# The front's products of a streaming-encoder layer: one fp32 matmul per product in place of three fp32r passes over split halves

## The chip, the cores and the metric

The kernel runs on one core of one Trainium2 chip. The metric is device time in microseconds of one execution; the runs shown are of one program on one core. TensorE does the matrix products, VectorE, ScalarE and GpSimd the elementwise work, and SyncE (SP) issues the loads. Times "at" some microsecond count from the first instruction of the profiled execution.

## What is computed

One layer of an encoder on 256 tokens of 1024 features, all in fp32:

```python
x = layer_norm(x, ln_in_g, ln_in_b)
h = x @ w_in[l] + b_in[l]                       # 1024 -> 5640 columns
fq, fk, fv, ff, hq, hf, hi, hg, gates = split_cols(h, IN_SIZES)
...
y_fox = from_heads(fox_o) @ w_fox_branch[l]     # attention with forget gates, 8 heads of 64
...
y_hgrn = o @ w_hgrn_branch[l]                   # gated linear recurrence, 8 heads of 64
g = jax.nn.sigmoid(gates)
mixed = (g[..., :D_MODEL] * y_fox + g[..., D_MODEL:] * y_hgrn) @ w_mix_out[l] + b_mix_out[l]
x = layer_norm(ALPHA * x + mixed, ln1_g[l], ln1_b[l])
y_moe = grouped_top2_moe(x, ...)                # 16 experts, two chosen for each token
x = layer_norm(ALPHA * x + y_moe, ln2_g[l], ln2_b[l])
```

## The kernel before, in words

**Two parts.** The front is everything up to the first norm and the router: the input products, the two branches and the output projection, with the token mixer's work in between. The experts follow, two at a time, 64 slots for the tokens of each. The experts' 201 MB of weights are loaded once, in the order of use, into every slot that comes free.

**Tiles of the front.** The front's weights are 15 tiles of 128 x 4096 (2 MB each), numbered by `KIND` and loaded into a ring of three slots (`load_front`, line 81); the last tile has a place of its own. A tile is eight units of 512 columns. Tiles of kind "tm" (0, 3, 6 on the input, 13 and 14 for the output) give tokens on partitions: the operand is stationary and 512 columns of weights move, for two halves of tokens, so a unit has two products. Tiles of kind "fm" (1, 2, 4, 5, 7 to 10 on the input) and "f4" (11 and 12, the branches) give features on partitions: 128 x 128 of weights are stationary and 256 tokens move, four products to a unit.

**Three passes.** `prep(u)` (line 154) splits a unit of weights: `hi` is its rounding to fp32r, by ScalarE (line 164; three units by VectorE, line 162), `lo` is what is left, by VectorE or GpSimd (line 165, chosen by `on_pool`). The operands are split in the same way: the input by `x_hi` and `x_lo` (lines 244 to 249), the branches' by `feat_split` and `f_split`, the output's by `mix_split`. A product is then three matmuls into one bank of PSUM (`mm`, lines 185 to 187 and 198 to 200). The cumulated forget gates (`f_sum`, lines 675 and 678) use the same trick.

**The order.** TensorE, VectorE, ScalarE and GpSimd run in the order of the code. The loop at line 1065 makes steps 2 to 59 of two units each: `pe[i]` before the step's first products, evacuations of finished products and `post[i]` after them, then `prep` for units ahead, then the second unit. `pe`, `mid` and `post` hold the mixer's work, put at its steps with `at`. Steps 8 to 11 are tile 2, steps 12 to 15 are tile 3, and so on. Steps 16 to 23 carry the recurrence, step 24 a branch on a value that all engines read (line 594), steps 29 to 40 the attention. VectorE evacuates tile 0 (`ev_hv`, line 374), which frees two of the four banks that products use, and tile 2 (`ev_hq`, line 384); for tile 1 it works on SBUF alone (lines 379 and 380). GpSimd prepares the residual in seven sweeps over 128 x 1024 (`resid`, lines 317 to 322), placed at steps 4 to 9.

**Loads.** SP issues loads in an order of its own, which the scheduler decides; a load waits for its slot. `load_front` is called for the next tile when a tile has been used (steps 3, 7, 11, ...), `load_exp` and `load_parts` for the experts. Slots for experts come free as the front goes on: four at steps 16 to 29, one at step 40, the mixer's operands at steps 48 and 52 (`phase5`, `phase6`), the gates' at step 53 (`phase7`), the ring's, and the input's and the last tile's from step 56 on (`last_parts`). `warm` and `warm1` are products without use, over waits.

Of the kernel before, what the change touches and what calls it, by code (L numbers as in the profile page):

```python
# [35 lines left out]
# columns of the row pack  # L36
# [10 lines left out]
def trunk(ctx: ExitStack, tc: tile.TileContext, x, cst_d, rows_d, wf, we, lvl_d, out):  # L47
# [98 lines left out]
    # ---- products in three passes of exact halves; a unit: 512 columns of a weight tile  # L146
    KIND = ["tm", "fm", "fm", "tm", "fm", "fm", "tm", "fm", "fm", "fm", "fm", "f4", "f4", "tm", "tm"]
    split = {}
    NU = 8 * len(KIND)

    def on_pool(u):
        return u in (0, 1, 2) or 24 <= u < 56 and u % 2 == 1 or u >= 56 and u % 4 == 3

    def prep(u):
        if u >= NU:
            return
        c = u % 8
        src = fr[u // 8][c // 2][:, c % 2 * 512:c % 2 * 512 + 512] if u >= NU - 8 else fr[u // 8][:, c * 512:c * 512 + 512]
        hi = HI.tile([128, 512], F32R, name="hi", tag="hi")
        lo = HI.tile([128, 512], F32R, name="lo", tag="lo")  # L160
        if u in (6, 28, 30):
            V.tensor_copy(hi, src)
        else:
            A.copy(hi, src)  # L164
        (G if on_pool(u) else V).tensor_sub(lo, src, hi.bitcast(F32))  # L165
        split[u] = hi, lo
# [5 lines left out]
    def mm(u, tts=(0, 1)):  # L172
        i, c = u // 8, u % 8
        hi, lo = split[u]
        rh, rl = operands[i]()
        if KIND[i] == "tm":
            for tt in tts:
                if c == 0:
                    # the very last sums in two banks, so that their ends can overlap
# [43 lines left out]
    def x_turn(tt, j):  # L223
        """two blocks of features, a bank each pair"""
# [6 lines left out]
    def x_affine(tt, j):  # L231
        p = xq[tt, j]
        if j == 0:
            xq["t", tt] = P2.tile([128, 8, 128], F32, name="xt", tag="hk" if tt else "lf")
        xt = xq["t", tt][:, 2 * j:2 * j + 2, :]
        for i in range(2):
            k = slice(2 * j + i, 2 * j + i + 1)
            if j % 2 == 0:
                V.tensor_scalar(xt[:, i, :], p[:, i, :], C("ing")[:, k], C("inb")[:, k], op0=OP.mult, op1=OP.add)
            else:  # L240
                A.activation(xt[:, i, :], p[:, i, :], AF.Identity, bias=C("inb")[:, k], scale=C("ing")[:, k])
        xq[tt, j] = xt

    def x_hi(tt, j):
        A.copy(xt4[j][:, 0, :, tt * 128:(tt + 1) * 128], xq[tt, j])

    def x_lo(tt, j):
        t = slice(tt * 128, (tt + 1) * 128)
        (G if j == 3 or (tt, j) == (1, 1) else V).tensor_sub(xt4[j][:, 1, :, t], xq[tt, j],
                                                             xt4[j][:, 0, :, t].bitcast(F32))  # L250

    operands = {i: (lambda: xp) for i in range(11)}
    def x_parts(tt, j):
        x_affine(tt, j)
        x_hi(tt, j)
        x_lo(tt, j)
# [11 lines left out]
    prep(0)  # L268
    prep(1)
    x_affine(0, 0)  # L270
    x_affine(0, 1)
    x_stats(1)
    x_hi(0, 0)
    x_hi(0, 1)
    x_lo(0, 0)
    mm(0, (0,))
    V.bn_aggr(mvs(1), sm[:, 24:36])
    x_lo(0, 1)
    mm(1, (0,))
    prep(2)  # L280
# [3 lines left out]
    prep(3)  # L284
    x_turn(1, 0)
    x_turn(1, 1)
    mm(2, (0,))
    mm(3, (0,))
    x_affine(1, 0)
    x_norm(1, 1)  # L290
    x_affine(1, 1)
    x_hi(1, 0)
    x_hi(1, 1)
    x_lo(1, 0)
    x_lo(1, 1)
    mm(0, (1,))
    x_turn(1, 2)
    x_turn(1, 3)
    mm(1, (1,))
    x_affine(0, 2)  # L300
    x_hi(0, 2)
    x_lo(0, 2)
    mm(2, (1,))
    prep(4)
    x_affine(1, 2)
    x_hi(1, 2)
    x_lo(1, 2)
    mm(3, (1,))
    prep(5)
    x_parts(0, 3)  # L310
    prep(6)
    x_parts(1, 3)
    prep(7)

    # residual with the output bias: alpha * (x * g + b) + b_mix
# [8 lines left out]
    # lower bounds of the forget gates: cumsum(softmax) - its first row, over one layer  # L324
# [4 lines left out]
    Ur = PB.tile([128, 256], F32R, name="ur")  # L329
# [25 lines left out]
    def small3():  # L355
        V.tensor_copy(Ur, U)

    # tensors of the mixer
# [48 lines left out]
    # ---- HGRN2  # L407
# [7 lines left out]
    def hgrn_general(oh):  # L415
        """the same scores for any decays: pairs of tokens by the highest bit in which they differ;
        every exponent is at most zero"""
# [3 lines left out]
        for j in range(4):  # L421
# [38 lines left out]
            # between chunks: from the end of the key's chunk to the start of the query's  # L460
# [43 lines left out]
    def h_exps(j):  # L504
# [7 lines left out]
        # half of the chunk's decay as the reference point: exponents of both signs, at most  # L512
        # half the decay; beyond SAFE the general path below recomputes the scores
# [6 lines left out]
        # between chunks: from the key's reference point to the query's  # L520
# [18 lines left out]
    # two heads side by side: each on its half of the tensor engine's rows  # L539
# [21 lines left out]
    def transposed(p, val, sts, j):  # L561
        """two heads' sums of values: features on partitions, the scores' keys there too"""
# [51 lines left out]
    def feat_pe(ot):  # L614
        """[tokens, 512] to features on partitions"""
# [5 lines left out]
    def feat_split(p, o, tt):  # L621
        t = slice(tt * 128, (tt + 1) * 128)
# [990 lines left out]
```

## Time and profile before

| | us |
|---|---|
| median of 3 runs | 703.58 |
| lowest and highest | 702.56, 705.85 |
| profiled execution, span from first to last instruction | 704.5 |
| TensorE busy | 661.4 (94%) |
| VectorE, ScalarE, GpSimd busy | 210.1, 188.5, 93.1 |
| read from HBM | 236.95 MB, 338 GB/s over the span |

Of the profiled execution the span is the only time on record, and it stands for that execution's own time below. Busy time of TensorE is the union of modelled durations, which overlap from one matmul to the next, so it says that an engine has work, not that it is at its peak. The chain of waits follows the end back to what released each step. Stretches with their busy times, the granted clock and the load queue's share tell the stages apart; a clock of 1.00 is 2.4 GHz and one of 0.50 is 1.2 GHz. "f32" stands for fp32 and fp32r alike in a matmul's shapes; the tiles' names tell them apart (`hi`, `lo`, `xp`, `mp` are fp32r).

### The profile page before, as it was taken

The page shows a single profiled execution, that of the slowest core. Times are in us where ns is not written, and L with a number is a line of the kernel's source. Part 1 is how long each engine was busy: PE and PEld are TensorE (multiplying, and loading weights), DVE is VectorE, ACT ScalarE, POOL GpSimd, SP SyncE. Part 2 cuts the span into 40 slices and gives each one's busy share as a digit, 9 for nine tenths or more (in the row PEclk, how much of TensorE's full clock was granted, in tenths as well). Part 3 has the DMA queues.
Part 4 walks back from the last instruction along what each step waited for, and adds up shares of the span by engine and source line. Part 5 has one row for each costly group of instructions (what it writes and reads, how often), then busy time and mean ns, then how long its engine had stood idle before and what let it go on. Part 6 is the DMA issues. An engine that isn't in the chain of part 4 may idle for free.

```text
span 704.5 us, 9357 instructions
## 1 busy us (share of the span) xinstructions
PE 661.4 (94%) x3707; PEld 388.1 (55%) x3707; DVE 210.1 (30%) x457; ACT 188.5 (27%) x389; POOL 93.1 (13%) x83
## 2 busy tenths in 40 slices
PE   6779998999999999999999999999999999699986
PEld 5678797899998953534534443443443433243433
DVE  5776862654468521100100100100100100100015
ACT  4536354577645421102012010010010010010211
POOL 2632344433136000000000000000000000000001
PEclk8979999999999999999999999999999999999999
DMA  8926633543978969999999999999999999999981
GB/s 330 382 105 225 270 121 123 194 178 118 360 287 300 397 206 375 425 394 429 425 407 424 421 412 421 424 412 421 420 417 419 418 420 416 418 425 410 412 331 60
DMA packets 40520, 238.75 MB, mean 339 GB/s; under 512 B 4496, under 2 KB 4624, under 8 KB 32400
## 3 DMA queue, kind: packets, MB, share of 16 engines
q1 hardware_dynamic: 40464, 238.02, 84.3%
q8 instruction: 33, 0.54, 0.3%
q14 instruction: 23, 0.19, 0.1%
HBM read 236.95 MB, written 1.05 MB: 338 GB/s over the span
## 4 chain that ended last, share of the span: by engine, by line
PE 67%; DMA 13%; DVE 2%; ACT 0%; issue 0%; DVEq 0%; SPq 0%; ACTq 0%
PE g L1276 25%; DMA w<-in_we_dram 13%; PE g L1293 13%; PE g L1248 3%; PE g L198 3%; PE g L199 3%; PE g L200 3%; PE acc L1301 3%; PE g L186 1%; PE g L187 1%; PE g L185 1%; PE g L1312 1%; PE g L1422 1%; PE g L1284 1%; PE g L1116 1%; DVE e L1465 1%
## 5 line engine op out<-in xcount | busy, mean ns | idle before, releaser
L1276 PE MATMUL g<-w,e 128*64 128x512 f32 x992 | 219.7, 595 | 2.4 <-DMA w<-in_we_dram 2.4
L1276 PEld LDWEIGHTS g<-w,e 128*64 128x64 f32 x992 | 69.0, 137 | 138.6 <-issue 125.8
L1293 PE MATMUL g<-w,f 128*64 128x512 f32 x448 | 106.5, 604 | 2.4 <-DMA w<-in_we_dram 2.4
L165 DVE TENSOR_TENSOR lo<-w,hi 128x512 fp32r<-128x512 f32 x85 | 69.1, 824 | 62.1 <-ACT hi L164 61.3
L164 ACT CAST hi<-w 128x512 fp32r<-128x512 f32 x117 | 70.4, 620 | 54.2 <-PE g L199 39.3
L198 PE MATMUL g<-xp,hi 128*128 128x256 f32 x256 | 76.3, 298 | 9.0 <-DVE hv L374 9.0
L199 PE MATMUL g<-xp,hi 128*128 128x256 f32 x256 | 74.2, 290 | 0.0
L200 PE MATMUL g<-xp,lo 128*128 128x256 f32 x256 | 74.0, 289 | 0.0
L1293 PEld LDWEIGHTS g<-w,f 128*64 128x64 f32 x448 | 39.2, 138 | 59.5 <-issue 54.5
L1523 POOL TENSOR_TENSOR e<-e,par 128x256 f32<-128x256 f32 x2 | 1.4, 726 | 459.4 <-DVE nmr L1519 459.4
L165 POOL TENSOR_TENSOR lo<-w,hi 128x512 fp32r<-128x512 f32 x35 | 47.4, 1357 | 109.6 <-ACT hi L164 109.6
L198 PEld LDWEIGHTS g<-xp,hi 128*128 128x128 f32 x256 | 50.8, 199 | 11.3 <-issue 10.4
L199 PEld LDWEIGHTS g<-xp,hi 128*128 128x128 f32 x256 | 50.9, 199 | 0.1
L200 PEld LDWEIGHTS g<-xp,lo 128*128 128x128 f32 x256 | 50.8, 199 | 0.0
L1479 DVE COPY f<-g 128x512 f32<-128x512 f32 x7 | 4.8, 692 | 115.2 <-PE g L1293 115.2
L1248 PEld LDWEIGHTS g<-e,raw 128*128 128x128 f32 x224 | 26.1, 191 | 19.8 <-DVE e L1240 10.0
L1248 PE MATMUL g<-e,raw 128*128 128x128 f32 x224 | 28.7, 281 | 8.1 <-DVE e L1240 8.1
L1259 ACT ACTIVATE e<-g,cst 128x128 f32<-128x128 f32 x28 | 10.6, 457 | 68.7 <-PE g L1248 68.7
L1463 DVE TENSOR_TENSOR e<-e,g 128x512 f32<-128x512 f32 x8 | 5.5, 688 | 73.5 <-ACT e L1462 73.5
L185 PE MATMUL g<-hi,xp 128*128 128x512 f32 x48 | 20.7, 431 | 6.5 <-PEq L594 3.4
L1471 ACT COPY f<-g 128x512 f32<-128x512 f32 x8 | 4.7, 586 | 79.9 <-PE g L1284 79.9
L1301 PE MATMUL acc<-f,e 128*128 128x512 f32 x56 | 25.9, 605 | 0.0
(318 smaller groups left out, 745.5 us busy)
## 6 DMA issues: line engine op xcount, KB each, us to landing
w<-in_we_dram SPq DMA_DIRECT2D x49, 2048.0 KB, 17.7
w<-in_we_dram SPq DMA_DIRECT2D x178, 512.0 KB, 10.4
w<-in_wf_dram SPq DMA_DIRECT2D x13, 2048.0 KB, 8.4
w<-in_wf_dram SPq DMA_DIRECT2D x8, 512.0 KB, 9.1
w<-in_we_dram SPq DMA_DIRECT2D x16, 256.0 KB, 6.0
rbc<-in_rows_dram SPq DMA_DIRECT2D x1, 1036.0 KB, 15.9
f<-in_we_dram SPq DMA_DIRECT2D x4, 256.0 KB, 7.6
out_dram<-par SPq DMA_DIRECT2D x4, 256.0 KB, 2.1
```

What stands on the lines that cost most here:

```text
L164: A.copy(hi, src)
L165: (G if on_pool(u) else V).tensor_sub(lo, src, hi.bitcast(F32))
L185: PE.matmul(p, rh(c)[:, t], hi[:, a:b], start=c == 0, stop=False, skip_group_check=True)
L186: PE.matmul(p, rh(c)[:, t], lo[:, a:b], start=False, stop=False, skip_group_check=True)
L198: PE.matmul(p, hi[:, w], rh(k), start=k == 0, stop=False)
L199: PE.matmul(p, hi[:, w], rl(k), start=False, stop=False)
L200: PE.matmul(p, lo[:, w], rh(k), start=False, stop=k == nk - 1)
L1248: PE.matmul(p[:, i, :], raw[:, tt, k * 128:(k + 1) * 128], oneh2[:, tt, :], start=tt == 0, stop=tt == 1)
L1259: A.activation(t[:, i, :], p[:, i, :], AF.Identity, bias=C("b1")[:, 4 + i:5 + i], scale=C("g1")[:, 4 + i:5 + i])
L1276: PE.matmul(h[64 * nh:64 * nh + 64, :], xg[kh][:, k, 64 * (e % 2):64 * (e % 2) + 64], wcol(e, m + kh, k, nh), start=kh + k == 0, stop=kh = ...
L1293: PE.matmul(py[nh][64 * a:64 * a + 64, :], hT[a][:, c0:c0 + 64], wt[:, nh * 512:nh * 512 + 512], start=f == 0, stop=f == 7)
L1301: PE.matmul(acc[tt][nh], GT[:, tt, :], y[nh], start=start, stop=False, skip_group_check=True)
```

## The change

Products take weights and operands as they are, in fp32, one matmul each. `prep`, `on_pool`, `halves`, `x_hi`, `x_lo`, `mix_split` and `small3` are gone. The normed input is written once, into two tiles (`xT`) instead of four. The branches' operands are one copy each (`feat_put`, `f_put`), and the output takes the gated sum where it lies, in `gates`. At the start, the second half of the tokens is prepared in one go, between the first four units' products for the first half and for the second. Everything else keeps its step.

```diff
     KIND = ["tm", "fm", "fm", "tm", "fm", "fm", "tm", "fm", "fm", "fm", "fm", "f4", "f4", "tm", "tm"]
...
-    def prep(u):
-        if u >= NU:
-            return
+    def wunit(u):
         c = u % 8
-        src = fr[u // 8][c // 2][:, c % 2 * 512:c % 2 * 512 + 512] if u >= NU - 8 else fr[u // 8][:, c * 512:c * 512 + 512]
-        hi = HI.tile([128, 512], F32R, name="hi", tag="hi")
-        lo = HI.tile([128, 512], F32R, name="lo", tag="lo")
-        if u in (6, 28, 30):
-            V.tensor_copy(hi, src)
-        else:
-            A.copy(hi, src)
-        (G if on_pool(u) else V).tensor_sub(lo, src, hi.bitcast(F32))
-        split[u] = hi, lo
+        return fr[u // 8][c // 2][:, c % 2 * 512:c % 2 * 512 + 512] if u >= NU - 8 else fr[u // 8][:, c * 512:c * 512 + 512]
...
                 for p, a in tmp[tt]:
-                    b = a + 512 // len(tmp[tt])
-                    PE.matmul(p, rh(c)[:, t], hi[:, a:b], start=c == 0, stop=False, skip_group_check=True)
-                    PE.matmul(p, rh(c)[:, t], lo[:, a:b], start=False, stop=False, skip_group_check=True)
-                    PE.matmul(p, rl(c)[:, t], hi[:, a:b], start=False, stop=c == 7, skip_group_check=True)
+                    PE.matmul(p, x_of(c)[:, t], w[:, a:a + 512 // len(tmp[tt])], start=c == 0, stop=c == 7,
+                              skip_group_check=True)
...
         for kk in range(4):
-            k, w = k0 + kk, slice(kk * 128, (kk + 1) * 128)
-            PE.matmul(p, hi[:, w], rh(k), start=k == 0, stop=False)
-            PE.matmul(p, hi[:, w], rl(k), start=False, stop=False)
-            PE.matmul(p, lo[:, w], rh(k), start=False, stop=k == nk - 1)
+            k = k0 + kk
+            PE.matmul(p, w[:, kk * 128:(kk + 1) * 128], x_of(k), start=k == 0, stop=k == nk - 1)
...
-    def halves(name):
-        """exact halves of eight blocks of features, in four parts"""
-        t = [X.tile([128, 2, 2, T], F32R, name=name, tag="w", bufs=4) for _ in range(4)]
-        return [lambda k, i=i: t[k // 2][:, i, k % 2, :] for i in range(2)], t
-
-    xp, xt4 = halves("xp")
+    xT = [X.tile([128, 4, T], F32, name="xT", tag="w", bufs=4) for _ in range(2)]
+
+    def x_of(k):
+        return xT[k // 4][:, k % 4, :]
...
     def f_sum(j):
...
-            for part in range(2):
-                PE.matmul(pF[:, hh], lfr[:, part, h:h + 1].to_broadcast([128, 128]), Ur,
-                          start=part == 0, stop=False)
-            for part in range(2):
-                PE.matmul(pF[:, hh, 1], lfr[:, part, 8 + h:9 + h].to_broadcast([128, 128]),
-                          Ur[:, 0:128], start=False, stop=part == 1)
+            PE.matmul(pF[:, hh], f[:, 2, h:h + 1].to_broadcast([128, 128]), U, start=True, stop=False)
+            PE.matmul(pF[:, hh, 1], f[:, 2, 8 + h:9 + h].to_broadcast([128, 128]), tri, start=False, stop=True)
...
-    operands[11] = lambda: [lambda k, i=i: oH[i][:, k, :] for i in "hl"]
-    operands[12] = lambda: [lambda k, i=i: oF[i][:, k, :] for i in "hl"]
-    operands[13] = operands[14] = lambda: late["mp"]
+    operands[11] = lambda k: oH["o"][:, k, :]
+    operands[12] = lambda k: oF["o"][:, k, :]
+    operands[13] = operands[14] = lambda k: late["gates"][:, k, :]
...
-        if i > 2:
-            prep(2 * i + 3)
...
-        prep(2 * i + 4)
```

How the instructions move, at three places. On TensorE, at the start (line 127 is `warm`, 228 and now 207 the turning of the input, `g`, `s`, `o` are banks), the first products of tile 0 stood before like this:

```order
L127 MATMUL s<-hst_116 128x128 x2
L185 MATMUL g<-hi,xp 128x512
L186 MATMUL g<-lo,xp 128x512
L187 MATMUL g<-hi,xp 128x512
L185 MATMUL g<-hi,xp 128x512
L186 MATMUL g<-lo,xp 128x512
L187 MATMUL g<-hi,xp 128x512
L228 MATMUL g<-cst,raw 128x128 x2
```

and now, up to the end of tile 2 (line 169 is a product of 512 columns, 181 one of 256, 566 and 577 belong to the forget gates):

```order
L127 MATMUL s<-hst_116 128x128 x2
L169 MATMUL g<-w,xT 128x512 x4
L207 MATMUL g<-cst,raw 128x128 x2
L207 MATMUL s<-cst,raw 128x128 x2
L207 MATMUL o<-cst,raw 128x128 x2
L207 MATMUL g<-cst,raw 128x128 x2
L169 MATMUL g<-w,xT 128x512 x12
L181 MATMUL g<-xT,w 128x256 x8
L566 MATMUL g<-xT,wff 32x128 x16
L181 MATMUL g<-xT,w 128x256 x8
L577 MATMUL g<-cst,ffs 128x128 x2
L181 MATMUL g<-xT,w 128x256 x48
```

Each triple has become one row's count, on `w` and `xT` themselves; the four turnings of the second half stand together.

On VectorE, around steps 4 to 8 (`lbt` are the lower bounds, `hv`, `lf`, `hk` the evacuations of tiles 0 and 1, `ff` the forget gates), before:

```order
L343 TENSOR_SCALAR lbt<-cst 128x4
L165 TENSOR_TENSOR lo<-w,hi 128x512 x2
L374 TENSOR_TENSOR hv<-g,rbc 128x512 x2
L165 TENSOR_TENSOR lo<-w,hi 128x512 x2
L379 TENSOR_SCALAR lf<-lf,lbt 128x256
L380 TENSOR_SCALAR hk<-hk,lbt 128x256
L165 TENSOR_TENSOR lo<-w,hi 128x512 x2
```

and now, up to the first evacuations of tile 2 (`hqt`):

```order
L276 TENSOR_SCALAR lbt<-cst 128x4
L304 TENSOR_TENSOR hv<-g,rbc 128x512 x2
L309 TENSOR_SCALAR lf<-lf,lbt 128x256
L310 TENSOR_SCALAR hk<-hk,lbt 128x256
L309 TENSOR_SCALAR lf<-lf,lbt 128x256
L310 TENSOR_SCALAR hk<-hk,lbt 128x256
L582 TENSOR_REDUCE ff<-g 128x16
L583 TENSOR_TENSOR ff<-ff,rbc 128x16
L585 TENSOR_SCALAR ff<-ff 128x16
L586 TENSOR_TENSOR ff<-ff 128x16
...
L314 SCALAR_TENSOR_TENSOR hqt<-g,cst,hqt 128x256 x4
```

The splits between the evacuations are gone; left out are four more rows of 309 and 310.

On SP, the loads after the third weight tile (128x4096 from `in_wf` is a front tile, `in_we` are experts' weights), before:

```order
L99 DMA in_bmix<-in_rows_dram 128x1024
L84 DMA w<-in_wf_dram 128x4096 x4
L891 DMA w<-in_we_dram 128x1024 x3
L84 DMA w<-in_wf_dram 128x4096
L891 DMA w<-in_we_dram 128x1024
L864 DMA w<-in_we_dram 128x4096
L84 DMA w<-in_wf_dram 128x4096 x2
```

and now:

```order
L99 DMA in_bmix<-in_rows_dram 128x1024
L84 DMA w<-in_wf_dram 128x4096 x2
L804 DMA w<-in_we_dram 128x1024
L84 DMA w<-in_wf_dram 128x4096
L804 DMA w<-in_we_dram 128x1024 x3
L777 DMA w<-in_we_dram 128x4096
L84 DMA w<-in_wf_dram 128x4096
L804 DMA w<-in_we_dram 128x1024 x2
L84 DMA w<-in_wf_dram 128x4096 x3
```

The first expert loads stand two front tiles earlier, and two parts more come before tile 6, in what the input's split halves used to take.

## Rows read from the trace of the kernel before

**Rows 1.** Page, the chain that ended last: shares of the span by engine.

```profile
PE 67%; DMA 13%; DVE 2%; ACT 0%; issue 0%; DVEq 0%; SPq 0%; ACTq 0%
```

**Rows 2.** The chain in order of time: start us, us, what.

```profile
251.09 1.87 PE g L1422 x8
...
589.55 10.18 DMA w<-in_we_dram
...
676.35 4.47 DMA w<-in_we_dram
```

**Rows 3.** By stretch: us; PE, PEld, DVE, ACT, POOL busy; clock, DMA share, GB/s.

```profile
0.00:32.00 32.00, 25.97 (x148) 21.14 (x148) 21.09 (x42) 18.45 (x38) 13.52 (x22) 0.89 0.92 363
32.00:63.50 31.50, 23.09 (x171) 23.12 (x172) 23.77 (x37) 12.27 (x25) 11.01 (x5) 0.84 0.36 135
63.50:181.00 117.50, 111.81 (x838) 100.10 (x836) 67.53 (x180) 71.05 (x158) 44.12 (x36) 0.97 0.50 187
181.00:239.30 58.30, 58.07 (x420) 54.43 (x419) 35.91 (x60) 29.03 (x50) 21.58 (x18) 1.00 0.85 324
239.30:282.00 42.70, 42.70 (x243) 23.27 (x243) 12.23 (x51) 10.55 (x18) 0.00 (x0) 0.96 0.83 310
282.00:590.00 308.00, 301.07 (x1432) 124.65 (x1430) 31.62 (x52) 33.04 (x73) 0.00 (x0) 1.00 1.02 418
```

**Rows 4.** TensorE in order of time, products of 256 columns.

```profile
189.73 0.28 PE L198 MATMUL g<-xp,hi 128*128 128x256 f32 x1
...
190.09 0.28 PE L198 MATMUL g<-xp,hi 128*128 128x256 f32 x1
```

**Rows 5.** TensorE in order of time, products of 512 columns; the last begins tile 3.

```profile
21.71 0.39 PE L185 MATMUL g<-hi,xp 128*128 128x512 f32 x1
...
22.39 0.39 PE L185 MATMUL g<-hi,xp 128*128 128x512 f32 x1
...
63.46 0.40 PE L185 MATMUL g<-hi,xp 128*128 128x512 f32 x1
```

**Rows 6.** TensorE in order of time, fp32 matmuls of the experts; x2 covers both.

```profile
311.36 0.59 PE L1301 MATMUL acc<-f,e 128*128 128x512 f32 x1
...
311.36 1.02 PE L1301 MATMUL acc<-f,e 128*128 128x512 f32 x2
...
689.12 0.70 PE L1319 MATMUL acc<-f,e 128*128 128x256 f32 x2
```

**Rows 7.** Groups by shape, TensorE: count, busy us, mean ns, idle before.

```profile
L198 PE MATMUL g<-xp,hi 128*128 128x256 f32 x256 | 76.3, 298 | 9.0 <-DVE hv L374 9.0
...
L185 PE MATMUL g<-hi,xp 128*128 128x512 f32 x48 | 20.7, 431 | 6.5 <-PEq L594 3.4 <-ACT xp L245 3.1
```

**Rows 8.** TensorE's waits up to 250 us: total, times, longest.

```profile
PE g L198 <- DVE hv L374: 9.0, 1, 9.0
PE g L185 <- PEq L594: 3.4, 1, 3.4
...
PE o L577 <- DVE hst L558: 1.5, 1, 1.5
...
PE g L186 <- DVE lo L165: 0.9, 2, 0.7
```

**Rows 9.** VectorE and GpSimd in order of time, during the residual's sweeps.

```profile
33.95 2.34 POOL L322 TENSOR_TENSOR raw<-raw,in_inb 128x1024 f32<-128x1024 f32 x1
34.01 2.31 DVE L343 TENSOR_SCALAR lbt<-cst 128x4 f32<-128x4 f32 x1
...
39.19 2.69 POOL L322 TENSOR_TENSOR raw<-raw,in_inb 128x1024 f32<-128x1024 f32 x1
```

**Rows 10.** Page, costliest groups: the splits of the weights.

```profile
L165 DVE TENSOR_TENSOR lo<-w,hi 128x512 fp32r<-128x512 f32 x85 | 69.1, 824 | 62.1 <-ACT hi L164 61.3
L164 ACT CAST hi<-w 128x512 fp32r<-128x512 f32 x117 | 70.4, 620 | 54.2 <-PE g L199 39.3
```

**Rows 11.** SP's waits up to 250 us.

```profile
SPq L84 <- DVE lo L165: 115.2, 10, 16.5
```

More of the change, by code (lines that the diff above doesn't have):

```diff
@@ L147, in trunk @@
     KIND = ["tm", "fm", "fm", "tm", "fm", "fm", "tm", "fm", "fm", "fm", "fm", "f4", "f4", "tm", "tm"]
-    split = {}
     NU = 8 * len(KIND)
-    def on_pool(u):
-        return u in (0, 1, 2) or 24 <= u < 56 and u % 2 == 1 or u >= 56 and u % 4 == 3
-    def prep(u):
-        if u >= NU:
-            return
-        c = u % 8
-        src = fr[u // 8][c // 2][:, c % 2 * 512:c % 2 * 512 + 512] if u >= NU - 8 else fr[u // 8][:, c * 512:c * 512 + 512]
-        hi = HI.tile([128, 512], F32R, name="hi", tag="hi")
-        lo = HI.tile([128, 512], F32R, name="lo", tag="lo")
-        if u in (6, 28, 30):
-            V.tensor_copy(hi, src)
-        else:
-            A.copy(hi, src)
-        (G if on_pool(u) else V).tensor_sub(lo, src, hi.bitcast(F32))
-        split[u] = hi, lo
+    def wunit(u):
+        c = u % 8
+        return fr[u // 8][c // 2][:, c % 2 * 512:c % 2 * 512 + 512] if u >= NU - 8 else fr[u // 8][:, c * 512:c * 512 + 512]
     tmp = {}
@@ L173, in mm @@
         i, c = u // 8, u % 8
-        hi, lo = split[u]
-        rh, rl = operands[i]()
+        w, x_of = wunit(u), operands[i]
         if KIND[i] == "tm":
@@ L231, in x_affine @@
     def x_affine(tt, j):
[L232 to L235, printed above, removed]
+        p = xq.pop((tt, j))
         for i in range(2):
-            k = slice(2 * j + i, 2 * j + i + 1)
+            k = 2 * j + i
+            t, c = x_of(k)[:, tt * 128:(tt + 1) * 128], slice(k, k + 1)
             if j % 2 == 0:
-                V.tensor_scalar(xt[:, i, :], p[:, i, :], C("ing")[:, k], C("inb")[:, k], op0=OP.mult, op1=OP.add)
+                V.tensor_scalar(t, p[:, i, :], C("ing")[:, c], C("inb")[:, c], op0=OP.mult, op1=OP.add)
             else:
[L241 to L256, printed above, removed]
+                A.activation(t, p[:, i, :], AF.Identity, bias=C("inb")[:, c], scale=C("ing")[:, c])
+    operands = {i: x_of for i in range(11)}
     x_stats(0)
@@ L267, in trunk @@
     warm(2, 128)
[L268 to L271, printed above, removed]
+    for j in range(4):
+        x_affine(0, j)
     x_stats(1)
[L273 to L276, printed above, removed]
     V.bn_aggr(mvs(1), sm[:, 24:36])
-    x_lo(0, 1)
-    mm(1, (0,))
-    prep(2)
     A.activation(mvs(1)[:, 1:2], mvs(1)[:, 1:2], AF.Sqrt, bias=eps_in[:, 0:1])
@@ L283, in trunk @@
     x_norm(1, 0)
[L284 to L289, printed above, removed]
-    x_norm(1, 1)
[L291 to L313, printed above, removed]
+    x_norm(1, 1)
+    for u in range(4):
+        mm(u, (0,))
+    for j in range(4):
+        x_turn(1, j)
+    for j in range(4):
+        x_affine(1, j)
+    for u in range(4):
+        mm(u, (1,))
     gA, bA, bM = inr
@@ L328, in trunk @@
     e0, e1 = lbt[:, 12:16], lbt[:, 16:20]
-    Ur = PB.tile([128, 256], F32R, name="ur")
     rst = P2.tile([128, T], F32, name="rst")
@@ L353, in small4 @@
         G.tensor_copy(wff[:, :, 0:8], C("wff").rearrange("p (k c) -> p k c", c=8))
-    def small3():
-        V.tensor_copy(Ur, U)
     def p4(dt=F32, shape=(128, 4, T)):
@@ L619, in feat_pe, with feat_put @@
         return p
-    def feat_split(p, o, tt):
-        t = slice(tt * 128, (tt + 1) * 128)
-        A.copy(o["h"][:, :, t], p)
-        V.tensor_sub(o["l"][:, :, t], p, o["h"][:, :, t].bitcast(F32))
+    def feat_put(p, o, tt):
+        A.copy(o[:, :, tt * 128:(tt + 1) * 128], p)
     F = {}
     f = const.tile([128, 3, 16], F32, name="ff")
-    lfr = const.tile([128, 2, 16], F32R, name="lfr")
     fs = const.tile([128, 56], F32, name="fs")
@@ L638, in f_proj @@
                 r = slice(32 * (k % 4), 32 * (k % 4) + 32)
-                PE.matmul(pf[r, tt * 128:(tt + 1) * 128], wff[:, k, :], xq["t", tt][:, k, :],
+                PE.matmul(pf[r, tt * 128:(tt + 1) * 128], wff[:, k, :], x_of(k)[:, tt * 128:(tt + 1) * 128],
                           start=k < 4, stop=k >= 4, skip_group_check=True)
@@ L665, in f_log2 @@
         V.tensor_add(f[:, 2, :], f[:, 2, :], f[:, 1, :])
-        V.tensor_copy(lfr[:, 0, :], f[:, 2, :])
-        V.tensor_sub(lfr[:, 1, :], f[:, 2, :], lfr[:, 0, :].bitcast(F32))
     def f_sum(j):
@@ L731, in f_out, with f_put @@
         transposed(F["o"][j // 2][:, j % 2, :], vt, [F.pop(("P", 2 * j + hh)) for hh in range(2)], j)
-    def f_split(i):
+    def f_put(i):
         if i == 0:
-            oF["h"], oF["l"] = p4(F32R), p4(F32R)
-        js = slice(2 * i, 2 * i + 2)
-        A.copy(oF["h"][:, js, :], F["o"][i])
-        V.tensor_sub(oF["l"][:, js, :], F["o"][i], oF["h"][:, js, :].bitcast(F32))
+            oF["o"] = p4()
+        A.copy(oF["o"][:, 2 * i:2 * i + 2, :], F["o"][i])
     def ev_gate(n):
@@ L760, in ev_fox @@
         G.tensor_add(g[:, b, :], g[:, b, :], g[:, 8 + b, :])
-    def mix_split(b):
-        g, t = late["gates"][:, b:b + 2, :], late["mt"][b // 2]
-        mh, ml = t[:, 0], t[:, 1]
-        A.copy(mh, g)
-        V.tensor_sub(ml, g, mh.bitcast(F32))
     rT = {}
@@ L916, in trunk @@
     at(post, 4, small2)
-    at(post, 9, small3)
     at(post, 3, small)
@@ L951, in h_feat_pe @@
         if tt == 0:
-            oH["h"], oH["l"] = p4(F32R), p4(F32R)
+            oH["o"] = p4()
         H["f", tt] = feat_pe(H["ot", tt])
     def h_feat(tt):
-        feat_split(H["f", tt], oH, tt)
+        feat_put(H["f", tt], oH["o"], tt)
     for tt in range(2):
@@ L993, in trunk @@
     at(post, 39, gate_bulk, 5, NID)
-    at(post, 38, f_split, 0)
-    at(post, 40, f_split, 1)
+    at(post, 38, f_put, 0)
+    at(post, 40, f_put, 1)
     def phase4():
@@ L1010, in trunk @@
     at(post, 40, phase4)
-    def mixed():
-        late["mp"], late["mt"] = halves("mp")
-    at(pe, 45, mixed)
-    for n in range(4):
-        at(post, 50 + n, mix_split, 2 * n)
     def phase5():
```

## Prediction

> **What bounds the kernel now.** I read the chain of waits first, because it says which engine's time becomes the end. Its shares [rows 1] put 67% on TensorE and 13% on loads of the experts' weights. The chain in order of time [rows 2] shows how these two divide the span: TensorE carries it up to 589.6 us, then back-to-back loads of expert weights do up to 680.8, and a short tail follows. So two things have to move together: the moment at which the experts begin (near 251 us), and the stream of loads that feeds them.
>
> The second view is the busy time by stretch [rows 3]. From 282 us on the load queue is full (share 1.02, 418 GB/s). Before 282 it is not: 32.0 x 363 + 31.5 x 135 + 117.5 x 187 + 58.3 x 324 + 42.7 x 310 GB/s is 70.0 MB, which at 418 GB/s would take 167 us of the 282. The stream has 115 us of slack, all of it in the front, and TensorE fills the front (112 of 117.5 us, 58.1 of 58.3). Whatever TensorE saves there starts the experts earlier; the stream can follow as long as the saving stays well under 115 us. The bytes are the same before and after.
>
> The third view is the order of time on TensorE inside the front. A product of 256 moving columns is three fp32r matmuls, and the first of the next product starts 0.36 us later, 0.12 us a pass [rows 4]. One of 512 columns takes 0.68 us [rows 5]. The durations in these rows (0.28 and 0.39 us) are longer than a pass because neighbours overlap; starts are what counts.
>
> **The change, part by part.** *Products.* Each triple becomes one fp32 matmul. Its price stands in the experts' part, where fp32 matmuls with 128 stationary columns already run beside a full load queue: one lasts 0.59 us and two in a row 1.02 us, so the second adds 0.43 us for 512 columns [rows 6]. For 256 columns I take 0.22 us, half of that and a little; the ends are 0.215, and 0.27, from the last rows of the kernel, where the second of two 256-column matmuls adds 0.70 less 0.43 at most [rows 6]. The Trainium skill speaks against this (FP8 and Floating Point Precision, TensorE Precision Notes): true FP32 takes four passes through the array, which would make one such matmul dearer than the three passes it replaces, and by it the sum would be 761 us instead of 634. The trace of this case does not agree: 0.43 us is under two passes of 0.23. The counts are 320 products of 256 columns (256 on the input, 64 in the branches) and 80 of 512 (48 on the input, 32 in the output, 8 of them cut in two); the rows show those on the input [rows 7], the code the others.
>
> I split the sum at 63.46 us, where the fourth weight tile (tile 3) begins [rows 5], because before that point the front waits for loads.
>
> *Up to tile 3.* What is queued up to and with the third weight tile is 10.5 MB by the code's sizes, and nothing of it moves. The queue carried 11.6 MB in the first 32 us at share 0.92 [rows 3], some of it the fourth tile's, so the third tile lands at about 32 us in either kernel. By then the changed kernel has done tiles 0 and 1: 16 x 0.43 + 32 x 0.22 = 14 us of products, 21 if the first tile runs at half clock. Tile 2 is 32 x 0.22 = 7 us: 39 us. Then a wait that I take from the stall of before. There TensorE stood 9.0 us for the evacuation of tile 0 [rows 8], because VectorE was late: an operation on 128x4 took 2.3 us and ended as a GpSimd sweep over 128x1024 ended [rows 9], and so with its neighbours. Those sweeps (the residual) stay where they are, up to 41.9 us, since they wait for loads that don't move. VectorE now does the tiny ones and the evacuation of tile 0 ahead of the sweeps, but 11 operations on SBUF stand between that and the first evacuation of tile 2, and a sweep lets one or two of them through. I put that evacuation at 42 to 43 and charge 4 us (ends: 0, and the 9.0 of before). Tile 3 then begins at 43 instead of 63.5: **20.5 us**.
>
> *Tiles 3 to 14.* 256 x (0.36 - 0.22) = 35.8 us, and 64 x (0.68 - 0.43) = 16.0 us: **51.8 us**. The forget gates' sums go from two passes of 0.12 and two of half the width to fp32 matmuls of 0.22 and 0.11, 8 times over: nothing that counts. The wait for a split weight, 0.9 us, goes; the wait of 3.4 us at the branch stays [rows 8].
>
> *Splits.* Gone are 70.4 us of ScalarE and 69.1 us of VectorE [rows 10], and GpSimd's third of the subtractions. I give them nothing: ScalarE and VectorE are under 62% busy in every stretch after 63.5 [rows 3], so they were cover, not bound. What remains of them lies under the products. What is late next is the mixer's handovers (scores, mask, output; scores, softmax, flip), which were spaced by steps of 2.9 us of products and now have 1.8: I charge 3 us, ends 0 and 24 (second rival).
>
> *Loads.* A ring slot was released by the last split of its tile, and the queue stood 115.2 us for that on VectorE [rows 11]; now TensorE's last matmul on the tile releases it, one or two steps later in the program but earlier in time. With three slots, a load of 2 MB (5 us at 418 GB/s) still has two tiles of at least 7 us each. Past 181 us it gets tight: 58.3 x 324 GB/s is 18.9 MB, 45 us of queue, for a stretch that shrinks to 58.3 - 13.4 - 8 = 37. Some 8 us of loads slip behind it, where 42.7 x 310 GB/s leaves 11 us of slack [rows 3]: free, if they are experts' weights and not the last front tiles. Freed early are half of the input's slots and two of the mixer's four; later by the length of the output products comes the gates' slot, whose 2 MB (weights of the second expert) are due some 25 us after the experts begin. I charge nothing for either.
>
> *Sum.* 20.5 + 51.8 + 0.9 - 3 = 70.2, and 704.5 - 70.2 = 634.3 for the profiled execution. Its span is 0.9 above the median of the runs: **633 us**.
>
> **The rivals.** *The handovers become the bound.* The mixer's chains cross three engines within a step or two, and 24 steps (16 to 39) carry them. For it: VectorE already stopped TensorE once here, 1.5 us at the first output [rows 8], and after each wait the granted clock can drop to half (mean 0.97 in 63.5 to 181, 0.84 in 32 to 63.5 [rows 3]). Against: with the splits gone, both engines have half their work. At 1 us a step it gives back 24 us: 657 us. *The waits vanish.* VectorE is early enough at tile 2 (4 us), no handover is late (3 us), the output's wait goes (1.5 us), half clock too (0.03 x 117.5 = 3.5 us), and 0.215 holds (1.4 us): 620 us. *Slower: fp32 costs four passes in the front.* If weights and operands straight from the loads made the matmul run as 4 x 0.12 and 4 x 0.23 us, the front would grow by 320 x 0.12 + 80 x 0.23 = 57 us: 761 us. It decides from 0.36 us per 256 columns, the price of three passes. Against it stands the same instruction at 0.43 us per 512 columns while the queue is full [rows 6, 3]; for it, that no row shows one with 256 columns in a long run. It is what the rule of the Trainium skill named above would do here. That the change doesn't do what it says is ruled out by the order of instructions: one matmul stands for three, and the splits are gone.
>
> **How the numbers follow.** Forecast 0.57, with its own range 622 to 645 (the 4 and 3 us at their ends, 0.23 instead of 0.22, the 8 us of loads falling on front tiles); late handovers 0.20; vanished waits 0.19; four passes 0.03; anything near no change 0.01. The range of 8 in 10 takes in most of the second and third: 615 to 656 us. A measurement of this kernel can tell about 0.5% from no change. Faster 0.96, same 0.01, slower 0.03.
>
> **What would show it.** In the changed kernel's order of time, products of the input start 0.22 us apart and those of the output 0.43; above 0.36 the slower rival holds. The third tile's first matmul stands near 32 us and the fourth's near 43; a wait there is on VectorE. The last product ends near 168 us instead of 239, and from there on the load queue stays full. TensorE's waits between 63 and 130 us say which of the first two rivals is nearer. I am wrong in kind if the experts begin 60 us earlier and the end does not move with them, or if front tiles are waited for after 32 us.

## The result, and the profile after

The changed kernel takes 728.64 us (median of 4 runs, 723.69 to 729.91) against 703.38 for the kernel before on the same chip (4 runs): a ratio of 1.033, 95% interval 1.028 to 1.038. It is slower by 25 us where 70 less were forecast. Its profiled execution took 729.91 us, with a span of 727.7.

The page of the changed kernel shows the cause in section 5, its costliest groups (line, engine, operation, tiles and shape, count; then busy us and mean ns of one, and idle time before them):

```profile
L181 PE MATMUL g<-xT,w 128*128 128x256 f32 x512 | 115.9, 382 | 0.0
L181 PEld LDWEIGHTS g<-xT,w 128*128 128x128 f32 x512 | 95.6, 190 | 14.9 <-issue 2.0
L169 PE MATMUL g<-w,xT 128*128 128x512 f32 x96 | 44.5, 616 | 6.4 <-issue 4.5
L181 PE MATMUL g<-p,w 128*128 128x256 f32 x128 | 27.8, 379 | 0.0
```

The input has 256 products of 256 columns and 48 of 512 [rows 7]. The rows count 512 and 96, and 512 weight loads. **One fp32 matmul of the program is two matmuls on TensorE, each with a weight load of its own.** TensorE in order of time (start us, us from start to end, group) gives the price of one such instruction:

```profile
54.33 1.45 PE L169 MATMUL g<-w,xT 128*128 128x512 f32 x3
```

```profile
201.41 0.38 PE L181 MATMUL g<-xT,w 128*128 128x256 f32 x1
201.62 1.46 PE L181 MATMUL g<-p,w 128*128 128x256 f32 x6
```

Three of 512 columns take 1.45 us and one lasts 0.59, as in [rows 6], so the starts are (1.45 - 0.59) / 2 = 0.43 us apart. Six of 256 columns take 1.46 and one 0.38: 0.216 apart. A product is two of them, 0.432 us and 0.86, where the kernel before has 0.36 and 0.68 [rows 4, 5]. These are 3.6 and 3.8 fp32r passes.

By stretch (us; busy PE, PEld, DVE, ACT, POOL; clock, DMA share, GB/s), as in [rows 3]:

```profile
0.00:32.00 32.00, 28.13 (x134) 18.57 (x135) 13.67 (x35) 9.26 (x19) 7.41 (x16) 1.00 0.94 364
32.00:63.50 31.50, 31.50 (x128) 23.79 (x127) 15.76 (x36) 9.69 (x23) 7.93 (x4) 1.00 0.80 315
63.50:181.00 117.50, 112.90 (x586) 85.96 (x585) 28.65 (x116) 33.53 (x86) 13.97 (x14) 0.99 0.38 139
181.00:239.30 58.30, 58.30 (x255) 46.65 (x254) 6.79 (x16) 6.63 (x12) 5.80 (x8) 1.00 0.65 253
239.30:282.00 42.70, 42.70 (x205) 30.55 (x206) 13.91 (x55) 8.18 (x15) 0.00 (x0) 0.88 0.61 218
282.00:590.00 308.00, 301.06 (x1444) 124.98 (x1442) 32.60 (x55) 35.22 (x76) 0.00 (x0) 1.00 1.01 415
```

VectorE and ScalarE fall to less than half of their busy time between 63.5 and 239.3, and TensorE does not follow: it is busy all through and waits for nothing that counts. All its waits up to the end of the front (us in total, times, longest):

```profile
PE g L169 <- issue: 4.5, 1, 4.5
PE g L169 <- DMA w<-in_wf_dram: 1.8, 2, 1.2
PE s L127 <- DVE eps L120: 1.3, 1, 1.3
PE g L207 <- DVE raw L198: 0.7, 1, 0.7
```

The 9.0 us behind the evacuation of tile 0 [rows 8] are gone; the stop of 4.5 us is the branch in the recurrence, 3.4 before. The chain of waits in order of time still goes over from TensorE to the loads, as in [rows 2], only later: the experts begin at 272.66 instead of 251.09, and the last load starts at 699.03 instead of 676.35.

```profile
272.66 1.87 PE g L1323 x8
...
699.03 4.94 DMA w<-in_we_dram
```

**The account.** Tile 3 begins at 54.33 us instead of 63.46 [rows 5]: 9.1 won. From there to the last product of the output the front takes 203.5 us, to 257.8, instead of 175.9, to 239.3: 27.6 lost. The prices say 256 x (0.432 - 0.36) + 64 x (0.858 - 0.68) = 29.8; less the waits of 1.5 and 0.9 us that went [rows 8], and 1.1 more at the branch, that is 28.5. The router loses 3.1 us more (granted clock 0.65 from 257.8 to 272.6 us, where the kernel before has 0.85 from 239.3 to 251), so the experts begin 21.6 us later. The load queue is full from 282 us on in both kernels, and the span ends 23.2 later.

### The profile page after: what moved, and what is told of

Same layout as the page of the kernel before. It is cut to its first block, busy times and chain, and to the rows that moved or that the text cites. A ratio compares the mean times of both kernels' runs of the same rounds, so it can differ in the third digit from the quotient of the medians.

```text
span 727.7 us, 8061 instructions
## 1 busy us (share of the span) xinstructions
PE 696.0 (96%) x3299; PEld 383.1 (53%) x3299; DVE 131.0 (18%) x353; ACT 117.8 (16%) x260; POOL 38.0 (5%) x45
## 4 chain that ended last, share of the span: by engine, by line
PE 62%; DMA 20%; DVE 1%; issue 1%; DVEq 0%; ACT 0%; SPq 0%
PE g L1177 20%; DMA w<-in_we_dram 20%; PE g L181 12%; PE g L1194 10%; PE g L169 5%; PE g L1149 3%; PE acc L1202 2%; PE g L1213 1%; PE g L1323 1%; PE g L1017 1%; PE g L1185 1%; PE g L1312 1%; PE acc L1220 1%; PE g L958 1%; PE acc L1085 0%
## 5 line engine op out<-in xcount | busy, mean ns | idle before, releaser
L181 PE MATMUL g<-xT,w 128*128 128x256 f32 x512 | 115.9, 382 | 0.0
L181 PEld LDWEIGHTS g<-xT,w 128*128 128x128 f32 x512 | 95.6, 190 | 14.9 <-issue 2.0
L169 PE MATMUL g<-w,xT 128*128 128x512 f32 x96 | 44.5, 616 | 6.4 <-issue 4.5
L169 PEld LDWEIGHTS g<-w,xT 128*128 128x128 f32 x96 | 18.4, 196 | 29.9 <-issue 28.8
L181 PE MATMUL g<-p,w 128*128 128x256 f32 x128 | 27.8, 379 | 0.0
L181 PEld LDWEIGHTS g<-p,w 128*128 128x128 f32 x128 | 24.4, 190 | 3.3
L169 PE MATMUL g<-w,gates 128*128 128x512 f32 (+1 forms) x64 | 25.4, 539 | 0.0
L1213 PE MATMUL g<-w,f 128*64 128x256 f32 (+1 forms) x96 | 16.3, 474 | 3.7 <-DMA w<-in_we_dram 3.7
L1202 PEld LDWEIGHTS acc<-f,e 128*128 128x128 f32 x56 | 10.1, 190 | 15.7 <-issue 15.7
L169 PEld LDWEIGHTS g<-w,gates 128*128 128x128 f32 x64 | 12.1, 190 | 11.8 <-issue 11.5
## 6 DMA issues: line engine op xcount, KB each, us to landing
w<-in_we_dram SPq DMA_DIRECT2D x178, 512.0 KB, 11.4
```

What stands on the lines that cost most here:

```text
L169: PE.matmul(p, x_of(c)[:, t], w[:, a:a + 512 // len(tmp[tt])], start=c == 0, stop=c == 7, skip_group_check=True)
L181: PE.matmul(p, w[:, kk * 128:(kk + 1) * 128], x_of(k), start=k == 0, stop=k == nk - 1)
L1202: PE.matmul(acc[tt][nh], GT[:, tt, :], y[nh], start=start, stop=False, skip_group_check=True)
L1213: PE.matmul(W["y"][64 * a:64 * a + 64, :], hT[a][:, c0:c0 + 64], w[:, 0:q], start=f == 0, stop=f == 7)
```

## The experiments

**The number of passes.** Theory: an fp32 product costs four passes, nothing else in the front matters, and at the price that was forecast the rest of the prediction would have come true. Rival: some other part of the new front (late operands, weights as loaded, slots) is slow. The changed kernel got each product as N one-pass bf16 matmuls on the upper halves of the same tiles, the second and later ones on a stationary tile of zeros:

```diff
+    def top(a):
+        return a.bitcast(BF)[:, 1::2]
...
-            PE.matmul(p, w[:, kk * 128:(kk + 1) * 128], x_of(k), start=k == 0, stop=k == nk - 1)
+            for j in range(N):
+                PE.matmul(p, zb if j else top(w[:, kk * 128:(kk + 1) * 128]), top(x_of(k)),
+                          start=k == 0 and j == 0, stop=k == nk - 1 and j == N - 1)
```

Products of the output, and of tiles 0, 3 and 6, likewise. What was expected of two and of four passes:

> The changed kernel with each product as two one-pass matmuls on the upper halves of the fp32 numbers (bf16, cut off), the second with zeros for the stationary operand; so the products keep only some 8 bits. A pass of 256 columns should start about 0.11 us after the one before, so a product costs 0.22 us, the price that the prediction took. Theory (the one wrong step is the price: an fp32 product is two instructions of 0.216 us, four passes in all, and everything else of the prediction holds): 320 x (0.22 - 0.43) + 80 x (0.43 - 0.86) = -102 us against the changed kernel's 728: 626 us, 615 to 645 with the waits that the prediction charged. Rival (the loss comes from loads that are issued later, since a slot is now held until the last product on it): 690 us or more.

> The same with four passes for a product (one on the upper halves, three with zeros). Theory: 4 x 0.11 = 0.44 us a product of 256 columns against 0.432 for the two fp32 instructions, 0.86 against 0.858 for 512 columns: 728 us, within 5. Rival (fp32 products cost something else beside their passes, such as a weight load that is not hidden): below 715.

Measured: 638.28 us with two (637.96 and 638.6) and 729.63 with four (726.99 and 732.27), beside 705.51 for the kernel before. By the medians four passes are the fp32 kernel within 1 us (the two runs are 5 us apart), and by another kind of instruction; two are within 5 us of the forecast 633. In the trace of two passes tile 3 begins at 40.84 us (43 was forecast), and the last product ends at 167.9 (168 was forecast). So of the prediction's sum the price of a product carries the miss. The smaller charges came out right in total and not in kind: the waits of 4 and 3 us did not come, and others of their size did (below). The groups of two passes show that here one row is one pass, 256 on the weights and 256 on zeros:

```profile
L191 PE MATMUL g<-xT,w 128*128 128x256 bf16 x256 | 61.0, 279 | 3.2 <-DMA w<-in_wf_dram 3.2
L191 PE MATMUL g<-xT,zb 128*128 128x256 bf16 x256 | 60.8, 279 | 0.0
```

Three passes and one, in a later comparison (before: 703.75):

> The changed kernel, each front product done as three one-pass matmuls: one on the upper bf16 halves of weight and operand, two more of the same shape on a stationary tile of zeros; the lower halves' share of the products is left out. Theory (what counts is the passes of a product, and nothing else in the front is late): the two-pass and four-pass forms were 638.3 and 729.6 us, 45.7 us for a pass, so 684 us (680 to 688). Against the kernel before (703.4), which also has three passes but splits its operands, that is about 19 less: some 9 of it up to tile 3, the rest from 0.33 in place of 0.36 us for a product. Rival (the splits cost TensorE nothing and three passes are three passes): within 4 us of the kernel before less the 9 won up to tile 3, 692 to 698.

> The changed kernel with one pass for each front product, on the upper bf16 halves of weight and operand; the lower halves' share of the products is left out. Theory A (the front's products set the end down to here): 638.3 - 45.7 = 592.6 us, 588 to 598. Theory B (below two passes the load queue, not TensorE, paces the front): some 237 MB at the 415 to 418 GB/s of the later stretches are 567 to 571 us, and with the some 23 us after the last load and 10 us at the start the time can't be under 600; 605 to 625 us. The second would say how far any cheaper product could have gone.

Measured: 676.11 us (675.91 to 678.63) and 615.91 (615.27 to 623.64). Three passes came out 8 us under the theory's 684, below its range, so time isn't even in the passes. The steps from four passes to one are 53.5, 37.8 and 22.4 us (the kernel before differs by 1.8 us between the two comparisons). A pass is 320 x 0.113 + 80 x 0.225 = 54 us of products, and the first step gives all of it. The later steps shrink in the front itself: its last product ends at 261.1, 207.4, 167.9 and 141.0 us, 53.7, 39.5 and 26.9 apart. With two passes TensorE waits for the third tile and stands at the recurrence's branch for 2.0 and 4.1 us, and its clock is 0.95 up to 63.5 us and 0.96 from there to 181, instead of 1.00 with three:

```profile
PE g L178 <- issue: 4.1, 1, 4.1
PE g L191 <- DMA w<-in_wf_dram: 3.2, 1, 3.2
PE g L178 <- PEq L535: 2.0, 1, 2.0
```

With three, the branch costs 1.6 us and the third tile nothing. Behind the front the loads take off little (53.5 of 53.7, 37.8 of 39.5, 22.4 of 26.9 arrive). By stretch, the queue with three passes is full from 239 us on; with two, from 181:

```profile
239.30:282.00 42.70, 41.57 (x198) 17.95 (x198) 4.80 (x8) 4.45 (x9) 0.00 (x0) 1.00 1.00 404
```

```profile
181.00:239.30 58.30, 57.17 (x284) 24.09 (x281) 8.39 (x24) 8.99 (x16) 0.00 (x0) 1.00 1.01 406
```

With one pass TensorE waits for the front's own weights, as theory B of that run has it:

```profile
PE g L178 <- DMA w<-in_wf_dram: 13.9, 2, 11.9
PE g L191 <- DMA w<-in_wf_dram: 8.9, 2, 5.2
```

The rival's 692 to 698 falls altogether. It took 9 us for the start, which is the gain with the dearer fp32 products in it; with three passes tile 3 begins at 45.21 us, 18.2 before the kernel before. From there to the front's end it is 162.2 us instead of 175.9; 4.2 of these 13.7 are waits (the branch at 1.6 instead of 3.4, and the 1.5 and 0.9 of [rows 8]), and some 5 can be the price of a product: three passes without splits run a tile of 32 products in 10.9 us, three with splits in 11.4 (tiles 11 and 12 of the two traces), so splits under the products cost TensorE at most 0.02 us a product, 5 us for the 256 products from tile 3 on. The rest of the 13.7 is not traced.

**The gates' slot.** The gated sum, now read in place, holds the slot of `gates` until the output is done. Copied into two other tiles at steps 50 to 53, it frees that slot at the same step as before; the copy takes two of the input's former slots in its place:

```diff
-    operands[13] = operands[14] = lambda k: late["gates"][:, k, :]
+    operands[13] = operands[14] = lambda k: late["mx"][k // 4][:, k % 4, :]
...
+    def mix_put(b):
+        A.copy(late["mx"][b // 4][:, b % 4:b % 4 + 2, :], late["gates"][:, b:b + 2, :])
```

> The changed kernel with the gated sum copied to a tile of its own for the output's products, so that the gates' slot takes its expert weights some 25 us earlier, as before. Theory (the price of the products alone): no change, 725 to 731 us. Rival (the gates' slot, released only by the last output product, holds back the stream of loads): 2 MB at 418 GB/s are 5 us, so 723 or less.

Measured: 726.56 us (724.88 to 730.59), 1.031 of the kernel before against 1.033 for the changed kernel. The intervals overlap; the experts begin at 272.32 instead of 272.66. The theory's band holds; the rival's 723 or less was not reached. The slot is not the cause of the 25 us.

**The start of the kernel before.** The prediction blamed VectorE's small operations under GpSimd's sweeps for the 9.0 us stall. In the kernel before, they were moved ahead of the sweeps:

```diff
+    small_a()
...
+    small_b()
...
-    at(post, 3, small)
```

> The kernel before with the lower bounds' tiny operations moved from step 3 into the start, ahead of the residual's sweeps on GpSimd. Theory (what the changed kernel won up to tile 3 is the 9.3 us stall behind VectorE, and that came from these operations waiting for the sweeps): the stall shrinks to 2 us or less, and the 10 us at half clock behind it go (5 us): 690 to 696 us. Rival (the evacuation of tile 0 is late for the splits ahead of it on VectorE): 700 to 704 us.

Measured: 701.19 us (699.41 to 702.89), ratio 0.993 (0.990 to 0.997): the rival's band, though not for its reason. The evacuation of tile 0 comes at 32.4 us and the stall is gone, but another takes its place. VectorE in order of time (the two L377 are the evacuation, L165 the splits), and TensorE's longest wait:

```profile
32.38 1.28 DVE L377 TENSOR_TENSOR hv<-g,rbc 128x512 f32<-128x512 f32 x2
33.58 4.48 DVE L165 TENSOR_TENSOR lo<-w,hi 128x512 fp32r<-128x512 f32 x2
```

```profile
PE g L200 <- DVE lo L165: 3.7, 1, 3.7
```

Two splits, SBUF to SBUF, take 4.48 us there, while GpSimd's sweeps of 2.7 and 2.8 us run; after the sweeps two take 1.28. The two evacuations, from PSUM, take 1.28 in the midst of a sweep. So the splits themselves are held back, and tile 3 begins at 59.25, not at 54.

**The changed kernel's start alone.** The kernel before with fp32 for tiles 0 to 2 (or for tile 0 alone), the input kept in the tiles that later hold the attention's queries and keys, and split once for the other tiles:

```diff
+    def x_of(k):
+        return (qT, kT)[k // 4][:, k % 4, :]
...
+        if i < 3:
+            w = fr[i][:, c * 512:c * 512 + 512]
...
+    def x_split(j):
+        src = (qT, kT)[j // 2][:, 2 * (j % 2):2 * (j % 2) + 2, :]
+        A.copy(xt4[j][:, 0], src)
+        V.tensor_sub(xt4[j][:, 1], src, xt4[j][:, 0].bitcast(F32))
```

> The kernel before with the changed kernel's start alone: tiles 0 to 2 are fp32 products on weights and input as loaded, the input is split at steps 7 to 10, and tiles 3 to 14 stay three fp32r passes. Theory (the change won some 9 us up to tile 3 by having no splits there, and lost from tile 3 on by the fp32 price alone): tile 3 starts at 54 to 56 us instead of 63.5, and the time is 703.4 - 9 = 694.5 us (691 to 697), less than either kernel. Rival (the splits for tile 3, under GpSimd's sweeps, are then what is late, or the loads set the end): 700 to 704.

> The kernel before with tile 0 alone as fp32 products on weights and input as loaded; the input is split whole behind tile 0's first products, and tiles 1 to 14 stay three fp32r passes. Theory (splits held back by GpSimd's sweeps cost the kernel before its start, as the earlier run with the moved small operations showed at 39.5 us): tile 1 starts near 25.3 as in the changed kernel, but tiles 1 and 2 wait for their splits, tile 3 starts at 56 to 61 us and the time is 696 to 701 us, behind the form with three fp32 tiles. Rival (only the value's evacuation was late): tiles 1 and 2 at 0.36 us for a product end at 48 to 50 us, and the time is 688 to 691, ahead of it.

Measured: 701.32 us (699.68 to 703.5) with three tiles, ratio 0.997 (0.9945 to 0.999); 699.63 (696.16 to 702.96) with one, ratio 0.994 (0.991 to 0.997). Both come out ahead of both kernels, but by about what can be told from no change. With one tile, tile 3 begins at 57.1 us and the time is in the theory's band, but not behind the form with three tiles, as the theory had it; with three the time is in the rival's, though not for the rival's causes. Its front did what was said: tile 3 begins at 53.07 and the front ends at 227.2 us, 12 before the kernel before. The gain went at the other end. TensorE stops behind the last expert's first half of columns, for nothing that the trace names, at the branch to the code for longer lists:

```profile
678.04 3.68 PE L1298 MATMUL g<-w,f 128*64 128x256 f32 x16 [9.60 <-issue]
```

**Without that branch.** Three kernels without it and the code in it:

```diff
-    over = nc.values_load(cfl, engines=(ET.PE, ET.Activation, ET.DVE, ET.Pool), min_val=0, max_val=1)
...
-    with tc.If(over > 0):
-        more_slots()
```

> The kernel before without the branch behind the last expert's first half of columns and without the code in it (the slots for lists longer than 64, which these tokens don't need). Theory (the branch costs TensorE time only where the last weights are there before it comes to it; in the kernel before it waits for a load there until 680.95 us): no change, 701 to 705 us. Rival (the branch costs its several us in every kernel): 694 to 700 us.

> The kernel before with the changed kernel's start (fp32 products for tiles 0 to 2), and without the branch behind the last expert's first half of columns and the code in it. Theory (the 9 us won at the start last through the loads, which end at 676 us instead of 685, and are then lost to the code behind the branch, at which TensorE stood 9.6 us without a wait): 703.8 - 9 = 695 us, 692 to 697, against 701.3 with the branch. Rival (the gain is lost to the loads themselves, or to a slower clock at the end): 699 to 702 us.

> The kernel before with tile 0 alone as fp32 products, and without the branch behind the last expert's first half of columns and the code in it. Theory (the branch held TensorE 4.0 us there, and the last weights came at 678 us instead of 685): 703.8 - 7 = 697 us, 695 to 698, against 699.6 with the branch. Rival (the branch costs nothing here): 699 to 701 us.

Measured: 697.60 (693.30 to 701.21), 689.43 (688.53 to 689.76) and 694.21 us (692.26 to 696.00), with the kernel before at 705.62 (ratios 0.988, 0.977, 0.984). For the kernel before, the rival held: the branch costs it 8 us too. The other two came out 2.6 and 0.8 us under their theories' ranges, which had given the branch no cost in the kernel before. That kernel's trace shows a wait for a load at that place, and slow products behind it (in the chain of waits):

```profile
PE g L1312 <- DMA w<-in_we_dram: 2.4, 1, 2.4
```

```profile
680.95 3.52 PE g L1312 x16
...
686.45 2.74 PE g L1312 x24
```

Sixteen rows take longer than the next 24; the granted clock is 0.52 from 681.0 to 684.4 us, about the level of 1.2 GHz, right behind the wait. Wait and clock make up some 4 of the 5.1 us by which the two traced executions differ (spans 704.5 and 699.4). The rest of the 8 us is not traced, and which part belongs to the read of the value, the jump or the code left out was not tried.

Without the branch the start's gain reaches the end: in the traces tile 3 begins at 52.14 us with three fp32 tiles instead of 63.40, the experts begin at 240.08 instead of 251.31, and the span is 688.0 instead of 699.4. By the medians it is less, 697.6 - 689.4 = 8.2 us, and 3.4 with one fp32 tile, where the spans differ by 7.0; the medians' intervals leave some 2 us either way. With the branch 2.4 of the 8.2 us are left for three tiles, but 4.1 for one (703.75 - 699.63): the branch swallowed most of the first gain and none of the second, whose stop there is 4.0 us instead of 9.6. The kernels without it drop a path that other inputs need, so they are no versions to use.

## Why the prediction was wrong

**The step that failed** is the price of a product: "one lasts 0.59 us and two in a row 1.02 us, so the second adds 0.43 us for 512 columns [rows 6]". The two in a row were the two halves of one matmul, and so were the two of 256 columns that gave the upper end, 0.27. The groups of the kernel before said so (TensorE, the rows of lines 1301 and 1319):

```profile
L1301 PE MATMUL acc<-f,e 128*128 128x512 f32 x56 | 25.9, 605 | 0.0
L1319 PE MATMUL acc<-f,e 128*128 128x256 f32 (+1 forms) x12 | 4.3, 482 | 0.5 <-ACT f L1314 0.5
```

Line 1319 stands in a loop over two halves of tokens and is called for three parts of the columns: 6 matmuls, and 12 rows. Line 1301 runs for seven pairs of experts, with four matmuls each: 28, and 56 rows. The order of instructions, which shows one row for each matmul of the program, did not reveal it. The price should have been 0.86 and 0.43 us, and the products' term 30 us lost instead of 51.8 won.

**The rule that was overruled** was right. The Trainium skill (FP8 and Floating Point Precision, TensorE Precision Notes) has four passes for true FP32; "the trace of this case does not agree" came from the same misread rows. With the price read rightly the trace agrees: 0.86 us is 3.8 fp32r passes, 0.432 us is 3.6, and four one-pass matmuls in place of one fp32 matmul give the same median within 1 us.

**The slower rival** had the mechanism and the point from which it decides (0.36 us for 256 columns), at a chance of 0.03. Its size was off in two terms. It priced 4 x 0.12 and 4 x 0.23 us, where 0.432 and 0.858 were measured: 320 x 0.072 + 80 x 0.178 = 37 us instead of 57. And it took no gain at the start into account, which was 9.1 us in spite of the dearer products of tiles 0 to 2. Of the 37 us, 29.8 fall on tiles 3 to 14; 29.8 - 9.1 = 20.7 us, and with the router's 3.1 and the changed waits (1.3 less) 22.5, beside 23.2 by the spans.

Point by point:

- *Up to tile 3*, 43 us forecast, 54.33 measured. Tiles 1 and 2 took 15.2 and 13.8 us instead of 7 each, by the price. The 4 us charged for a late evacuation did not come: TensorE is busy for 31.50 of the 31.50 us up to 63.5. At two passes tile 3 began at 40.84, inside the ends that the step gave (39 to 48).
- *VectorE under the sweeps* was the cause of the old stall, as the step says, but only the first in line: with it moved, the splits were late by 3.7 us. It took the whole change of the start to win the 9 us of the account, 18 at equal passes.
- *Splits at nothing* holds nearly: the splits under the products cost TensorE at most 0.02 us a product, 5 us from tile 3 on. With two passes that part took 127.1 us, beside the forecast's 125.
- *Handovers*, 3 us: the changed kernel, whose products are longer than before, does not try them. With two passes, at the price that was forecast, TensorE's longest waits in the front are for something else: 6.1 us at the recurrence's branch in two stops, and 3.2 at once and 3.4 in three waits for weights.
- *Loads* follow, as forecast: full from 282 us, and the end moves with the experts' beginning, 23.2 us for 21.6. The slack was there too: from four passes to two the end moved by 91 us where the front's end moved by 93. The tightness that the step saw in the front's last weights shows as a wait of 1.8 us for the output's weights with two passes, and of 11.9 with one.

## What to carry to other kernels

Before a row's duration is taken as the price of an instruction, hold its count against the number of times that the program issues it: a count that is double means that the price is double. If a rule speaks against a change, and one pair of rows speaks for it, that pair deserves a second view of its own (here the groups' counts) before the rule is given 3 in 100. And a gain at one end of a kernel is worth what the other end lets through: here, with a branch behind the last expert, 2.4 of 8.2 us were left of one early start, though all of a smaller one.

## What the runs showed of the hardware

- An fp32 matmul runs as two matmul instructions and two weight loads, each of 0.216 us for 256 columns and 0.43 for 512; a one-pass bf16 matmul of 256 columns, every second half-word of an fp32 tile read as its operand, keeps 0.11 us (the starts at 204.76 and 204.87 in the trace with four passes):

```profile
204.76 0.28 PE L191 MATMUL g<-p,zb 128*128 128x256 bf16 x1
204.87 0.27 PE L191 MATMUL g<-p,w 128*128 128x256 bf16 x1
```

- A VectorE operation from SBUF to SBUF that starts under a GpSimd sweep over 128x1024 can be held until the sweep ends, whatever its size: in the changed kernel 2.14 us for 128x16 and 2.43 for 128x256, where after the sweeps the latter takes 0.35. Not every operation is held: in the kernel before, a reciprocal of 128x4 took 0.18 us at 29.27, under a sweep that ran from 29.18 to 31.57. Evacuations from PSUM were not held (the two of 1.28 us above). In the changed kernel, VectorE and then GpSimd:

```profile
35.38 2.43 DVE L310 TENSOR_SCALAR hk<-hk,lbt 128x256 f32<-128x256 f32 x1
...
37.98 2.14 DVE L583 TENSOR_TENSOR ff<-ff,rbc 128x16 f32<-128x16 f32 x1
...
42.27 0.35 DVE L310 TENSOR_SCALAR hk<-hk,lbt 128x256 f32<-128x256 f32 x1
```

```profile
35.27 2.40 POOL L255 TENSOR_TENSOR raw<-raw,in_ing 128x1024 f32<-128x1024 f32 x1
37.74 2.34 POOL L256 TENSOR_TENSOR raw<-raw,in_inb 128x1024 f32<-128x1024 f32 x1
```

In the kernel before:

```profile
29.18 2.39 POOL L319 TENSOR_TENSOR in_inb<-in_inb,in_bmix 128x1024 f32<-128x1024 f32 x1
29.27 0.18 DVE L339 RECIPROCAL lbt<-lbt 128x4 f32<-128x4 f32 x1
```

- A branch that is not taken, with the read of its value and the code in it, cost 8 us (705.62 against 697.60), in a place where the trace shows a wait of 2.4 us for a load, or, with an earlier front, a stop of 9.6 without a cause. Around that stop, from 664 to 680 us, the DMA queues of the kernel with three fp32 tiles carry instructions as well as weights (packets, MB, share; the same queue has one packet there without the branch):

```profile
q1 hardware_dynamic: 2210, 4.12, 71.4%
q8 instruction: 3, 0.05, 1.2%
```

The Trainium skill (Runtime: NRT & Kernel Launch, Instruction fetch mechanics) has a taken branch whose target isn't among the instructions at hand wait for a transfer of them. If passing over the If's body is such a jump, that fits these rows and the runs without the branch; no run here shows that it is, nor which part of the stop the transfer makes up.
